# Hybrid attention and RWKV block: attention in steps of one segment, output products six steps back, every fifth full segment transposed by TensorE

## The chip, the cores and the metric

The kernel runs on one core of a Trainium2 chip. The metric is the device time of one execution in microseconds, lower is better. The core's engines work in parallel, each through its own queue in order: TensorE (PE, whose weight loads show as PEld), VectorE (DVE), ScalarE (ACT), GpSimd (POOL), and SyncE (SP), which here only issues transfers. ACT and POOL issue transfers too, and the 16 DMA engines carry all of them.

## What is computed

One block over 4096 tokens plus 16 meta tokens, with 8 attention heads of width 64 beside 8 RWKV-7 heads, then an output projection and a norm. The attention part of the reference, shortened:

```python
s = einsum('bhqd,bhkd->bhqk', q, k) / sqrt(64) + cq[..., :, None] - ck[..., None, :]
s = where(k_pos <= q_pos, s, NEG_INF)
o = einsum('bhqk,bhkd->bhqd', softmax(s), v)     # per block of 128 queries
y_fox = o * silu(z)
h = h + concatenate([y_fox, y_rwkv]) @ w_out     # then the final RMSNorm
```

## The kernel before

The program has two parts. In the **first part** the RWKV recurrence runs in 129 chunks of 32 tokens, three hops each. After each hop some of the input projections are put in as filler: a generator `fill` goes through four passes over the 16 blocks of 256 tokens (pass 0 makes the RWKV inputs, pass 1 the Q, K, V and gate of head pair 2, pass 2 those of pairs 0 and 1, pass 3 those of pair 3 and the RWKV gate). Each hop adds `RATE` = 0.33 to a credit; a yield of the generator costs 0.25 for 12 matmuls of 256 columns, so one unit is 48 such matmuls (`ps_in`, `ps_qk`, `ps_vz`, `ps_zr`).

In the **second part** the heads run in the order `HEADS`. A head has 32 rows of 128 queries; row i sees W = 16 + 128(i+1) keys, cut into segments of `SEG` = 1024. That makes 52 full segments and 32 shorter ones per head, 416 and 256 in all. For each segment:

1. PE makes the scores in a PSUM tile `ps_q` (two buffers): two matmuls of up to 512 columns for the high and low half of Q, and a mask product on the diagonal.
2. DVE adds the forget bias and takes the running maximum, into `sp` (fp32, L1051).
3. When all segments of the row have their maximum, ACT takes the exponential in place (L1065) and copies it to fp16, the high half of `hl` (L1071). POOL or DVE, by `POOL_SHARE` = 60 in 100, subtracts to get the low half (L1076).
4. SP issues a DMA transpose of `hl` (128 x 2048 fp16 for a full segment) into `ht` (L1078).
5. PE multiplies each 128 keys of `ht` with V: one matmul of 128 columns and one of 64, in `ps_o`.

`advance` takes one row at a time: all scores of row n, then all output products of row n-1 (`finish`), then steps 3 and 4 for all segments of row n. The buffers are 9 of `sp`, 6 of `hl` and 6 of `ht`. Between rows the rest of the filler is put in, in proportion to work done: what is left of `fill` counts in units, then `rwkv_out` (32 rows of 24 matmuls of 512 columns, `ps_p`) counts 0.5 a row. During head 7 the output projection and norm of finished rows run (`out_prep`, `out_rows`, again 24 `ps_p` matmuls a row).

A scheduler sets the order in every queue from priorities (`PR`) and its own model of time; an engine's queue is in order on the chip. `Ordered` can pin an instruction behind another one: in mode "note" it remembers the last instruction, in mode "behind" it adds an order-only dependency on it.

Of the kernel before, what the change touches and what calls it, by code (L numbers as in the profile page):

```python
# [40 lines left out]
NHL, NSP = 6, 9  # L41
HEADS = (4, 5, 0, 1, 2, 3, 6, 7)
POOL_SHARE = 60
# [4 lines left out]
RATE = 0.33  # L48
LEAD = 6
PARTS = ((0, 0), (0, 1), (1, 0))  # L50
# [26 lines left out]
def hymba_kernel(ctx: ExitStack, tc, x, meta, norm_w, w_in, b_f, mu_shift, w0, w_up, a0, a_up,  # L77
# [884 lines left out]
    with ExitStack() as fs:  # L962
# [18 lines left out]
        def projected(p, t):  # L981

            while done[PASS_OF[p]] * NB < min(t, SEQ + 1):
                next(late)
# [26 lines left out]
        nseg = 0  # L1011
        qz = {}

        def attention(h, i, head, dst):

            nonlocal nseg
            p, hp = divmod(h, 2)
            q0 = 64 * hp
            if i % 4 == 0:
                g = min(4, NT - i)  # L1020
                t0 = N_META + i * P
                projected(p, t0 + g * P)
                Q = at.tile([P, 2, 4 * P], F16, tag="Q", name="Q")
                for a in range(2):
                    DQ.dma_start(Q[64 * a:64 * a + 64, :, :g * P],
                                 qk_d[p][a:a + 2, q0:q0 + 64, t0:t0 + g * P].rearrange("v p t -> p v t"))
                Zt = at.tile([P, 4, HD], F32, tag="Z", name="Zt")
                DQ.dma_start(Zt[:, :g], zf_d[p][t0:t0 + g * P, q0:q0 + 64].rearrange("(s t) e -> t s e", t=P))
                qz[h] = (Q, Zt)
            Q, Zt = qz[h]  # L1030
            W = N_META + P * (i + 1)
            qs = slice((i % 4) * P, (i % 4) * P + P)
            sps = []
            mt = at.tile([P, 8], F32, tag="mt", name="mt", bufs=4)
            ni = 0
            for a0 in range(0, W, SEG):
                sp = at.tile([P, SEG], F32, tag="sp", name="sp", bufs=NSP)
                sps.append(sp)
                for a in range(a0, min(a0 + SEG, W), 1024):
                    b = min(a + 1024, W)  # L1040
                    c, o = chunk(a)
                    o = a - o
                    ps = ps_q.tile([P, 1024], F32, tag="q", name="ps_q")
                    for a2 in range(a, b, 512):
                        b2 = min(a2 + 512, b)
                        dg = max(a2, min(b2, W - P))
                        for v in range(2):
                            mm(ps[:, a2 - a:b2 - a], Q[:, v, qs], head[c][0][:, a2 - o:b2 - o], v == 0, v == 1 and dg == b2)
                        if dg < b2:
                            mm(ps[:, dg - a:b2 - a], identb, dmask[:, dg - W + P:b2 - W + P], False, True)  # L1050
                    V.tensor_tensor_reduce(out=sp[:, a - a0:b - a0], in0=ps[:, :b - a], in1=head[c][2][:, a - o:b - o],  # L1051
                                           scale=scs[:, p, 0, hp:hp + 1],
                                           scalar=(-3e38 if ni == 0 else mt[:, ni - 1:ni]),
                                           op0=ALU.add, op1=ALU.max, accum_out=mt[:, ni:ni + 1])
                    ni += 1
            nm = at.tile([P, 8], F32, tag="nm", name="nm", bufs=8)
            V.tensor_scalar(out=nm[:, 0:1], in0=mt[:, ni - 1:ni], scalar1=-1.0, scalar2=P_SHIFT,  # L1057
                            op0=ALU.mult, op1=ALU.add)
            yield
            hts = []  # L1060
            for a in range(0, W, SEG):
                b = min(a + SEG, W)
                n = b - a
                sp = sps[a // SEG]
                A.activation(sp[:, :n], sp[:, :n], AF.Exp, bias=nm[:, 0:1], accum_out=nm[:, 1 + a // SEG:2 + a // SEG])  # L1065
                nt = -(-n // P)
                hl = at.tile([P, 2 * SEG], F16, tag="hl", name="hl", bufs=NHL)[:, :2 * nt * P]
                hl3 = hl.rearrange("p (a k) -> p a k", a=2)
                if n % P:
                    G.memset(hl3[:, :, n:], 0.0)  # L1070
                A.activation(hl3[:, 0, :n], sp[:, :n], AF.Copy)  # L1071
                eng = V
                if n > P:
                    nseg += 1
                    eng = G if nseg * POOL_SHARE % 100 < POOL_SHARE else V
                eng.tensor_tensor(out=hl3[:, 1, :n], in0=sp[:, :n], in1=hl3[:, 0, :n], op=ALU.subtract)  # L1076
                ht = at.tile([P, 2 * SEG // P, P], F16, tag="ht", name="ht", bufs=NHL)[:, :2 * nt]
                SP.dma_start_transpose(out=ht, in_=hl)  # L1078
                hts.append(ht)
            yield  # L1080
            pso = ps_o.tile([P, P], F32, tag="o", name="ps_o")
            for a, ht in zip(range(0, W, SEG), hts):
                b = min(a + SEG, W)
                n = b - a
                nt = -(-n // P)
                for j in range(nt):
                    k = min(P, n - j * P)
                    jt = a // P + j
                    c, o = chunk(a + j * P)
                    Vj = head[c][1][:, o // P]  # L1090
                    first, last = jt == 0, b == W and j == nt - 1
                    mm(pso, ht[:k, j], Vj[:k], first, False)
                    mm(pso[:, 0:HD], ht[:k, nt + j], Vj[:k, 0:HD], False, last)
            ns = len(sps)
            if ns > 1:
                V.tensor_reduce(out=nm[:, 1:2], in_=nm[:, 1:1 + ns], axis=mybir.AxisListType.X, op=ALU.add)
            V.reciprocal(nm[:, 7:8], nm[:, 1:2])
            o1 = at.tile([P, HD], F32, tag="o1", name="o1", bufs=4)
            A.activation(o1, pso[:, HD:], AF.Copy)
            V.tensor_tensor(out=o1, in0=pso[:, 0:HD], in1=o1, op=ALU.add)  # L1100
            V.scalar_tensor_tensor(out=dst, in0=o1, scalar=nm[:, 7:8], in1=Zt[:, i % 4],
                                   op0=ALU.mult, op1=ALU.mult)
            yield

        heads = {h: {} for h in range(8)}
        need = lambda i: chunk(N_META + P * (i + 1) - 1)[0]

        def fetch(x, i):

            for (xx, ii) in ((x, i), (x, min(i + 3, NT - 1)), (min(x + (i + 6) // NT, 7), (i + 6) % NT)):  # L1110
                for c in range(need(ii) + 1):
                    if c not in heads[HEADS[xx]]:
                        heads[HEADS[xx]][c] = head_load(HEADS[xx], c)

        def out_weights(ow, k0):

            OH = ow.tile([P, 4, D], F32R, name="OH")
            OL = ow.tile([P, 4, D], F32R, name="OL")
# [167 lines left out]
```

## Time and profile before

| | |
|---|---|
| time, median of 3 runs (lowest to highest) | 4504.49 us (4469.48 to 4522.03) |
| the profiled execution: its time, and its span | 4462.28 us, 4460.4 us |
| busy over the span: PE, DVE, ACT, POOL | 88%, 66%, 48%, 50% |
| mean granted TensorE clock | 0.916 of full speed |
| full segments and shorter segments of attention | 416 and 256 |
| DMA transposes `ht<-hl` | 672 |

The span is that of one profiled execution, and the rows below are of that one. The last matmul of the recurrence (`psz`) starts at 1982 us and the first score (`ps_q`) at 2122 us, so these cut the program into its parts; the last score starts at 4319 us. Busy PE time counts each matmul from its start to its modelled end, so matmuls that follow each other closely overlap. A DMA share is packet time over 16 engines' time, and packets of several queues overlap, so it can pass 1.

### The profile page before, as it was taken

What the parts mean: (1) busy time and instruction counts of PE and PEld (TensorE: products, weight loads), DVE (VectorE), ACT (ScalarE), POOL (GpSimd) and SP (SyncE); (2) the same over time, 40 slices, a digit from 0 to 9 for tenths busy, and PEclk for the clock granted to TensorE, in tenths of its full rate; (3) what the DMA queues carried; (4) which work ended last, traced back from release to release, by engine and by line L of the source; (5) the groups of instructions that cost most, each with busy time, mean ns of one, the idle gap of its engine ahead of it and who ended that gap; (6) DMA issues with size and microseconds to landing.
All of it is one profiled execution on the core that took longest, in us unless ns stands there. A gap on an engine that the chain in (4) does not pass through costs nothing. (4 is left out here: it accounts for less than half of the span.)

```text
span 4460.4 us, 106426 instructions
## 1 busy us (share of the span) xinstructions
PE 3912.1 (88%) x42336; PEld 3012.8 (68%) x42336; DVE 2956.9 (66%) x6217; ACT 2122.7 (48%) x4338; POOL 2230.5 (50%) x3289
## 2 busy tenths in 40 slices
PE   5689999999989899998878878888888878978888
PEld 4577777777767677777656655666666656666566
DVE  5346665666667666752878978677787758646774
ACT  5433333333333233321666757577676747524552
POOL 4137565667666665762445545444454435332340
PEclk8899999999876899899999989999999989989989
DMA  9963223323222344324999999999999999999995
GB/s 265 262 172 93 79 79 97 87 75 90 74 70 79 85 138 121 98 88 141 196 213 229 216 193 227 199 216 227 208 212 234 212 203 223 258 270 242 198 218 185
DMA packets 1702644, 755.37 MB, mean 169 GB/s; under 512 B 1444601, under 2 KB 1639601, under 8 KB 1692162
## 3 DMA queue, kind: packets, MB, share of 16 engines
q1 hardware_dynamic: 1489346, 502.84, 55.8%
q10 hardware_dynamic: 194624, 170.08, 15.3%
q0 software_dynamic: 18176, 75.66, 5.6%
q8 instruction: 332, 5.44, 0.5%
q14 instruction: 166, 1.36, 0.1%
HBM read 278.97 MB, written 158.50 MB: 98 GB/s over the span
## 5 line engine op out<-in xcount | busy, mean ns | idle before, releaser
L1076 POOL TENSOR_TENSOR hl<-sp,hl 128x1024 f16<-128x1024 f32 (+7 forms) x384 | 719.7, 1881 | 517.3 <-ACT hl L1071 440.7
L1065 ACT ACTIVATE sp<-sp,nm 128x1024 f32<-128x1024 f32 (+8 forms) x672 | 644.5, 962 | 223.5 <-DVE nm L1057 175.6
L1071 ACT ACTIVATE hl<-sp 128x1024 f16<-128x1024 f32 (+8 forms) x672 | 568.2, 872 | 366.1 <-DMA ht<-hl 239.4
L92 PE MATMUL ps_o<-Vt,ht 128*128 128x64 f16 (+3 forms) x8960 | 559.5, 211 | 180.6 <-DMA ht<-hl 177.8
L92 PE MATMUL ps_q<-K,Q 128*128 128x512 f16 (+4 forms) x2432 | 596.9, 366 | 119.4 <-DVE mt L1051 118.3
L758 POOL TENSOR_TENSOR tm<-X,Am 128x248 f32<-128x248 f32 (+30 forms) x1023 | 498.1, 487 | 376.6 <-DMA Am<-a_d 290.1
L92 PEld LDWEIGHTS <-ht 128*128 128x128 f16 (+1 forms) x8960 | 466.9, 100 | 315.0 <-DMA ht<-hl 204.9
L92 PEld LDWEIGHTS <-wu 128*128 128x128 f16 (+1 forms) x5476 | 513.1, 102 | 194.8 <-ACT wu L160 28.1
L760 POOL TENSOR_TENSOR X<-X,tm 128x248 f32<-128x248 f32 (+30 forms) x1023 | 517.7, 506 | 76.6
L67 PEld LDWEIGHTS <-wu 128*128 128x128 f16 (+1 forms) x4988 | 454.5, 101 | 114.3 <-issue 26.0
L1051 DVE CUSTOM_DVE_ANT_0 sp<-ps_q,cb,mt 128x1024 f32<-128x1024 f32 (+8 forms) x416 | 436.1, 1048 | 80.3 <-PE ps_q L92 40.8
L1076 DVE TENSOR_TENSOR hl<-sp,hl 128x1024 f16<-128x1024 f32 (+8 forms) x288 | 383.2, 1333 | 99.3 <-ACT hl L1071 98.1
L92 PEld LDWEIGHTS <-Q 128*128 128x128 f16 x2432 | 221.8, 100 | 294.8 <-issue 150.2
L67 PE MATMUL ps_in<-fu,wu 128*128 128x256 f16 x3108 | 416.0, 285 | 3.4 <-DVE car L67 3.4
L1051 DVE CUSTOM_DVE_ANT_0 sp<-ps_q,cb,scs 128x1024 f32<-128x1024 f32 (+7 forms) x256 | 297.6, 1164 | 71.2 <-POOL hl L1076 43.9
L92 PE MATMUL ps_qk<-fu,wu 128*128 128x256 f16 x1632 | 237.7, 280 | 24.0 <-DVE t1k L500 18.5
L92 PE MATMUL ps_vz<-wu,fu 128*128 128x256 f16 x1644 | 247.6, 284 | 1.0 <-ACT th L544 0.6
L92 PE MATMUL ps_p<-OH,yH 128*128 128x512 f32 x512 | 221.5, 433 | 29.0 <-DVE oxt L1144 27.5
L1070 POOL MEMSET hl<- 128x224 f16 x256 | 72.4, 287 | 336.8 <-DMA ht<-hl 318.4
L92 PE MATMUL ps_zr<-fu,wu 128*128 128x256 f16 x1536 | 224.8, 285 | 8.0 <-DVE nm L1057 6.3
L67 PE MATMUL psz<-UV,SC 32*64 32x64 f32 (+1 forms) x4128 | 222.4, 232 | 3.0 <-ACT UV L67 2.2
L92 PE MATMUL ps_p<-OH,yL 128*128 128x512 f32 x512 | 209.6, 411 | 0.0
(350 smaller groups left out, 6976.6 us busy)
## 6 DMA issues: line engine op xcount, KB each, us to landing
fu<-u_d POOLq DMA_DIRECT2D x32, 1024.0 KB, 6.8
fu<-u_d SPq DMA_DIRECT2D x30, 1024.0 KB
pr<-p_d SPq DMA_DIRECT2D x32, 832.0 KB
p_d<-prt SPq DMA_DIRECT2D x96, 256.0 KB
u_d<-u SPq DMA_DIRECT2D x16, 1024.0 KB
Am<-a_d SPq DMA_DIRECT2D x128, 128.0 KB
Q<-qk_d ACTq DMA_DIRECT2D x128, 128.0 KB
oxt<-in_x_dram ACTq DMA_DIRECT2D x32, 512.0 KB
```

The lines of the kernel that those rows point to most:

```text
L67: r = f(*args, **kw)
L92: PE.matmul(o, lhsT=l, rhs=r, start=start, stop=stop)
L758: G.tensor_tensor(out=tm[:, :, :k], in0=bc(X[:, :, s:s + 1], [P, 8, k]), in1=bc(Am[:, s * C + s + 1:s * C + C].unsqueeze(1), [P, 8, k]), o ...
L760: G.tensor_tensor(out=X[:, :, s + 1:], in0=X[:, :, s + 1:], in1=tm[:, :, :k], op=ALU.add)
L1051: V.tensor_tensor_reduce(out=sp[:, a - a0:b - a0], in0=ps[:, :b - a], in1=head[c][2][:, a - o:b - o], scale=scs[:, p, 0, hp:hp + 1], scala ...
L1065: A.activation(sp[:, :n], sp[:, :n], AF.Exp, bias=nm[:, 0:1], accum_out=nm[:, 1 + a // SEG:2 + a // SEG])
L1070: G.memset(hl3[:, :, n:], 0.0)
L1071: A.activation(hl3[:, 0, :n], sp[:, :n], AF.Copy)
L1076: eng.tensor_tensor(out=hl3[:, 1, :n], in0=sp[:, :n], in1=hl3[:, 0, :n], op=ALU.subtract)
```

## The change

- Attention goes in steps of one segment. Step (n, sg) makes the scores of segment sg of row n+1, then the weights (exponential, split, transpose) of segment sg of row n, and then the output products of the segment that stands `LAG` = 6 steps back in a list `pend`.
- PE's order is tied: the first output matmul of a step is pinned behind the last score matmul.
- Of the full segments every fifth (`PE_SHARE` = 20) is not split into `hl` and not transposed by DMA. PE transposes its fp32 weights from `sp` in eight pieces of 128 x 128 into a `ps_q` buffer (`ps_w`); ACT copies the high half out to `ht`, and DVE subtracts for the low half.
- `RATE` falls from 0.33 to 0.265; 4 units of filler (`AHEAD`) go ahead of attention; `rwkv_out` counts 1.0 a row, not 0.5, and fill that a head forces is counted as spent.
- Buffers: `sp` 9 to 7, `hl` 6 to 5, `ht` 6 to 9, `nm` 8 to 12, `o1` 4 to 2, `Zt` 2 to 3. The share of POOL in the subtractions goes from 60 to 75 in 100. Q of the next four rows is loaded two rows ahead. Rows of the output projection follow what `pend` has finished.

```diff
-NHL, NSP = 6, 9
+NHL, NSP, NHT = 5, 7, 9
+PE_SHARE = 20
-POOL_SHARE = 60
+POOL_SHARE = 75
+AHEAD = 4
-RATE = 0.33
+RATE = 0.265
+LAG = 6
...
+        def weights(n, sg):
...
+            A.activation(sp[:, :nn], sp[:, :nn], AF.Exp, bias=nm[:, 0:1], accum_out=nm[:, 1 + sg:2 + sg])
+            ht = at.tile([P, 2 * SEG // P, P], F16, tag="ht", name="ht", bufs=NHT)[:, :2 * nt]
+            r["hts"].append(ht)
+            if nn == SEG:
+                npe += PE_SHARE
+                if npe >= 100:
+                    npe -= 100
+                    pt = ps_q.tile([P, nt, P], F32, tag="q", name="ps_w")
+                    for j in range(nt):
+                        PE.transpose(pt[:, j], sp[:, j * P:(j + 1) * P], ident)
+                    A.activation(ht[:, :nt], pt, AF.Copy)
+                    V.tensor_tensor(out=ht[:, nt:], in0=pt, in1=ht[:, :nt], op=ALU.subtract)
+                    return
...
+        def output(n, sg):
...
+            PE.mode = "behind"
+            for j in range(nt):
...
+                mm(pso, ht[:k, j], Vj[:k], jt == 0, False)
+                PE.mode = None
+                mm(pso[:, 0:HD], ht[:k, nt + j], Vj[:k, 0:HD], False, jt * P + k == W)
...
-                    yield 0.5
+                    yield 1.0
...
+        def pipeline():
+
+            for n in range(-1, len(steps)):
+                ka = segs(n) if n >= 0 else 0
+                kb = segs(n + 1) if n + 1 < len(steps) else 0
+                for sg in range(max(ka, kb)):
+                    if sg < kb:
+                        PE.mode = "note"
+                        scores(n + 1, sg)
+                        PE.mode = None
+                    if sg < ka:
+                        weights(n, sg)
+                        pend.append((n, sg))
+                    while len(pend) > LAG or pend and pend[0][0] < n - 4 or (n == len(steps) - 1 and sg == ka - 1 and pend):
+                        output(*pend.pop(0))
+                    if sg < ka:
+                        yield n, min(SEG, width_of(steps[n][1]) - sg * SEG) + 2 * P // ka
...
+        with tc.high_priority(offset=PR[5]):
+            while spent < AHEAD:
+                spent += next(late)
+        while now < 7 * NT:
+            with tc.high_priority(offset=PR[3]):
+                now, cols = next(att)
+            work += cols
+            with tc.high_priority(offset=PR[5]):
+                while spent * allwork < work * left:
```

Two places in the built program. First, ACT's queue where the recurrence gives way to attention: `qk`, `vt` and `t1k` end filler units, `Yt` ends the last RWKV rows, and the DMA rows load the first heads' K, bias, V and Q. Before:

```order
L67 ACTIVATE vt<-ps_vz 128x4x64
L67 ACTIVATE t1k<-t1k 128x256
L67 ACTIVATE qk<-ps_qk,sqs 128x256
L67 ACTIVATE qk<-ps_qk 128x256
L492 ACTIVATE vt<-ps_vz 128x4x64
L891 ACTIVATE Yt<-psd,gbT,gwT 128x32 x4
L502 ACTIVATE t1k<-t1k 128x256
L995 DMA K<-qk_d_102 64x1024 x3
L995 DMA K<-qk_d_102 64x1040
```

And in the changed kernel at the same place:

```order
L882 ACTIVATE sqd<-Y 32x512
L495 ACTIVATE vt<-ps_vz 128x4x64
L70 ACTIVATE wu<-wst 128x8x128
L505 ACTIVATE t1k<-t1k 128x256
L894 ACTIVATE Yt<-psd,gbT,gwT 128x32 x4
L999 DMA K<-qk_d_102 64x1024 x2
L1001 DMA cb<-c_d 128x1024
L1005 DMA Vt<-v_d_106 128x8x128
L1043 DMA Q<-qk_d_102 64x2x512 x4
L1045 DMA Zt<-zf_d_110 128x4x64 x3
L999 DMA K<-qk_d_102 64x1024 x2
```

The long run of filler ahead of `Yt` is gone: on PE 1074 `ps_qk` and `ps_vz` matmuls stand between the last `psz` and the first `ps_q` before, 120 now. Ahead of the last `psz` stand 2040 before and 1704 now, behind the first `ps_q` (with `ps_zr`) 4950 before and 6240 now. After the last `ps_q` stand 420 `ps_p` before and 300 now.

Second, PE in head 0 at the row of 1024 + 144 keys: score matmuls are `ps_q`, output products `ps_o`, and `fu` weights belong to filler. Before:

```order
L92 LDWEIGHTS Q
L92 MATMUL ps_q<-K,Q 128x512
L92 LDWEIGHTS Q
L92 MATMUL ps_q<-K,Q 128x144
L92 LDWEIGHTS Q
L92 MATMUL ps_q<-K,Q 128x144
L92 LDWEIGHTS ht
L92 MATMUL ps_o<-Vt,ht 128x128
L92 LDWEIGHTS identb
L92 MATMUL ps_q<-dmask,identb 128x128
L92 LDWEIGHTS ht
L92 MATMUL ps_o<-Vt,ht 128x64
```

And now, around the first segment that PE transposes:

```order
L1105 MATMUL ps_w<-ident,sp 128x128
L70 LDWEIGHTS Q
L70 MATMUL ps_q<-K,Q 128x512
L70 LDWEIGHTS Q
L70 MATMUL ps_q<-K,Q 128x512
L70 LDWEIGHTS Q
L70 MATMUL ps_q<-K,Q 128x144
L70 LDWEIGHTS Q
L70 MATMUL ps_q<-K,Q 128x144
L70 LDWEIGHTS identb
L70 MATMUL ps_q<-dmask,identb 128x128
L1105 MATMUL ps_w<-ident,sp 128x128 x7
```

Output products no longer stand among the matmuls of one score segment. The first of the eight transposes stands ahead of the next scores, the other seven behind them. In all 83 segments go this way (664 `ps_w`), and SP issues 589 transposes instead of 672.

## Rows read from the trace of the kernel before

**Rows 1.** The page: span, and busy time by engine (share, instructions).

```profile
span 4460.4 us, 106426 instructions
PE 3912.1 (88%) x42336; PEld 3012.8 (68%) x42336; DVE 2956.9 (66%) x6217; ACT 2122.7 (48%) x4338; POOL 2230.5 (50%) x3289
```

**Rows 2.** Busy by stage: from:to, length, busy (instructions), PE clock, DMA share, GB/s.

```profile
core 0: us, PE busy (x) PEld busy (x) DVE busy (x) ACT busy (x) POOL busy (x), PEclk, DMA share, GB/s
300.00:1982.00 1682.00, 1615.57 (x20914) 1269.92 (x20915) 1079.23 (x2363) 551.06 (x1374) 1111.51 (x2188) 0.91 0.32 89
1982.00:2122.00 140.00, 121.02 (x1097) 107.01 (x1094) 37.94 (x99) 20.80 (x53) 38.77 (x60) 0.93 0.45 140
2122.00:2833.00 711.00, 589.52 (x6240) 431.57 (x6238) 595.85 (x1251) 490.89 (x932) 363.28 (x343) 0.93 1.12 213
2833.00:3593.00 760.00, 661.32 (x6877) 499.02 (x6876) 563.29 (x1202) 509.24 (x1003) 352.67 (x330) 0.94 1.15 217
3593.00:3926.00 333.00, 270.30 (x2317) 197.77 (x2314) 216.77 (x438) 182.74 (x350) 134.21 (x116) 0.90 1.14 224
3926.00:4319.00 393.00, 330.61 (x2343) 242.25 (x2342) 250.88 (x482) 193.65 (x352) 132.67 (x110) 0.92 1.09 235
4319.00:4461.00 142.00, 119.53 (x649) 94.80 (x647) 72.47 (x106) 39.32 (x71) 21.88 (x25) 0.94 0.63 194
```

**Rows 3.** DMA queues, 2122 to 4461: packets, MB, share; an issue with its count.

```profile
q1 hardware_dynamic: 1168384, 293.69, 73.7%
q10 hardware_dynamic: 179408, 158.23, 27.2%
q0 software_dynamic: 13568, 55.79, 8.3%
...
fu<-u_d POOLq DMA_DIRECT2D x23, 1024.0 KB, 7.8
```

**Rows 4.** PE's waits, 2122 to 4461: for whom, us in total, times, longest.

```profile
PE ps_o L92 <- DMA ht<-hl: 177.8, 87, 11.0
PE ps_q L92 <- DVE mt L1051: 118.3, 104, 7.1
PE ps_p L92 <- DVE oxt L1144: 27.5, 19, 5.4
```

**Rows 5.** PE and ACT in order of time, 1982 to 2122: start, us, work, count.

```profile
1993.77 5.40 PE L67 MATMUL ps_vz<-wu,fu 128*128 128x256 f16 x48
...
2112.83 4.30 PE L92 MATMUL ps_qk<-fu,wu 128*128 128x256 f16 x20 [18.50 <-DVE t1k L500]
...
2084.62 8.52 ACTq L995 DMA_DIRECT2D K<-qk_d  x10
...
2109.76 1.17 ACTq L1028 DMA_DIRECT2D Zt<-zf_d  x2
```

**Rows 6.** PE in order of time, inside head 3.

```profile
3013.64 1.03 PE L92 MATMUL ps_q<-K,Q 128*128 128x512 f16 x4
...
3016.24 0.84 PE L92 MATMUL ps_o<-Vt,ht 128*128 128x128 f16 x16
```

**Rows 7.** The chain that ended last: one row of the output projection.

```profile
4414.67 5.72 PE ps_p L92 x24
```

**Rows 8.** The fp32 transposes that the kernel already has, with what empties them: ns min/median/max.

```profile
L1233 PE MATMUL ps_t<-ident,yf x128: 269/273/476, 4090.1 to 4440.7; 128*128 128x128 f32 x128
L1129 ACT ACTIVATE yH<-ps_t x32: 571/597/600, 4091.2 to 4441.0; 128x512 fp32r<-128x512 f32 x32
L1130 DVE TENSOR_TENSOR yL<-ps_t,yH x32: 671/691/693, 4091.8 to 4441.6; 128x512 fp32r<-128x512 f32 x32
...
4090.08 1.09 PE L1233 MATMUL ps_t<-ident,yf 128*128 128x128 f32 x4 [3.26 <-issue]
...
4420.23 0.60 PE L1233 MATMUL ps_t<-ident,yf 128*128 128x128 f32 x4
```

**Rows 9.** Groups by line and form, 2122 to 4461: busy us, mean ns, idle before.

```profile
L1076 POOL TENSOR_TENSOR hl<-sp,hl 128x1024 f16<-128x1024 f32 x240 | 532.6, 2223 | 412.3 <-ACT hl L1071 338.6 <-issue 29.8 <-DMA fnw<-in_final_norm_w_dram 19.6
L1065 ACT ACTIVATE sp<-sp,nm 128x1024 f32<-128x1024 f32 x416 | 473.6, 1140 | 172.0 <-DVE nm L1057 144.5 <-DVE ss L181 4.3 <-DMA out_dram<-oxt 4.2
...
L1051 DVE CUSTOM_DVE_ANT_0 sp<-ps_q,cb,mt 128x1024 f32<-128x1024 f32 x216 | 289.1, 1339 | 41.1 <-PE ps_q L92 27.8 <-POOL hl L1076 4.6 <-DVE mt L1051 3.0
L1076 DVE TENSOR_TENSOR hl<-sp,hl 128x1024 f16<-128x1024 f32 x176 | 271.5, 1543 | 53.3 <-ACT hl L1071 52.4 <-DMA Zt<-zf_d 0.6
```

More of the change, by code (lines that the diff above doesn't have):

```diff
@@ L981, in projected @@
         def projected(p, t):
+            nonlocal spent
             while done[PASS_OF[p]] * NB < min(t, SEQ + 1):
-                next(late)
+                spent += next(late)
         def head_load(h, c):
@@ L1009, in chunk @@
             return c, x - c * CH
[L1011 to L1103, printed above, removed]
@@ L1105, in hymba_kernel @@
+        nseg, npe, spent = 0, 0, 0
+        steps = [(hx, i) for hx in range(8) for i in range(NT)]
+        rows = {}
+        width_of = lambda i: N_META + P * (i + 1)
+        segs = lambda n: -(-width_of(steps[n][1]) // SEG)
+        qz, yos = {}, {}
         heads = {h: {} for h in range(8)}
-        need = lambda i: chunk(N_META + P * (i + 1) - 1)[0]
+        need = lambda i: chunk(width_of(i) - 1)[0]
         def fetch(x, i):
@@ L1169, in filler @@
                 for _ in rwkv_out(op, OW):
[L1170 to L1173 removed]
+                    yield 1.0
+        left = sum(max(0, NFULL - done[i]) * n for i, n in ((1, 2), (2, 4), (3, 4))) + NT
         late = filler()
[L1175 to L1189 removed]
@@ L1191, in advance @@
-        def advance(hx, i):
-            nonlocal before, yo
-            h = HEADS[hx]
-            fetch(hx, i)
-            if i % 4 == 0:
-                yo = at.tile([P, 4, HD], F32, tag="yo", name="yo")
-            gen = attention(h, i, heads[h], yo[:, i % 4])
-            next(gen)
-            finish()
-            next(gen)
-            before = h, i, gen, yo
-        yo = None
-        for hx in range(7):
-            for i in range(NT):
-                with tc.high_priority(offset=PR[3]):
-                    advance(hx, i)
-                work += i + 2
-                with tc.high_priority(offset=PR[5]):
-                    while spent * 7 * NT * (NT + 3) < work * 2 * total:
-                        cost = next(late, None)
-                        if cost is None:
-                            break
-                        spent += cost
+        pend = []
@@ new lines, in hymba_kernel @@
+        att = pipeline()
+        work, now = 0, -1
+        allwork = 7 * sum(width_of(i) + 2 * P for i in range(NT))
+        with tc.high_priority(offset=PR[5]):
+            while spent < AHEAD:
+                spent += next(late)
+        while now < 7 * NT:
[4 more added lines that the diff above has]
+                while spent * allwork < work * left:
+                    cost = next(late, None)
+                    if cost is None:
+                        break
+                    spent += cost
```

146 lines of the change are left out of this document (119 added, 27 removed).

## The prediction

> **What bounds the kernel now.** I read the page's shares first, then the stages, then inside attention PE's waits and the DMA queues. The page gives PE 88% of the span and every other engine 66% or less [rows 1]. That is an average over two parts with different limits. In the first part, 300 to 1982 us, PE is busy 1615.6 of 1682 us (96%) while the DMA engines stand at 0.32 [rows 2]: PE bounds it. From 1982 to 2122 us PE is busy 121.0 us with nothing but projections, DVE 37.9 and ACT 20.8: a seam in which attention hasn't begun. From 2122 us to the end PE is busy 83%, 87%, 81%, 84% and 84% of the five stages, while the DMA share is 1.09 to 1.15 until 4319 us. DVE is next, 1699 us of 2338 in sum (73%).
>
> Busy time there hides holes, since it counts the drain after each run of matmuls. So I count PE's work by pitch. A full segment's scores are four matmuls, 1.03 us with some 0.17 us of drain, so 0.86 us; 128 keys of output products are 0.084 us (16 matmuls, 0.84 us, the same drain) [rows 6]; a filler matmul is 0.109 us (48 in 5.40 us) [rows 5]; a row of the output projection 5.72 us [rows 7]. By the loops: scores 416 x 0.86 = 358, and 256 shorter segments at some 0.45 (464 columns twice, and the mask) = 115; products 4480 x 0.084 = 376; filler 4950 x 0.109 = 540; `rwkv_out` and output projection 64 x 5.72 = 366; small transposes 15. Sum 1770 us of the 2338. Named waits are 177.8 us of products for the transposes `ht<-hl`, 118.3 us of scores for DVE, which frees the two `ps_q` buffers, and 27.5 us of the output projection [rows 4], 324 in all. The other 244 us are mostly the half-speed clock: 0.93 granted over 2338 us is some 160 us, the rest small holes. The DMA engines are close behind: `q1`, nearly all of it transposes, holds 73.7% alone [rows 3].
>
> **The change, part by part.** *First part.* Ahead of the last `psz` 2040 `qk`/`vz` matmuls fall to 1704. 336 x 0.109 = 37 us, on the path because PE is 96% busy. Bounds: 0, if the recurrence's own hops set the pace, and 73 us at half speed (20 in 4.30 us, 0.215 each [rows 5]). I take -37.
>
> *Seam.* 1074 matmuls fall to 120: 954 x 0.109 = 104 us. What stays is ACT's queue. It issues 27 loads for the first heads from 2084.6 to 2110.9 us [rows 5], and PE then waits 18.5 us for what is queued behind them on ACT. The change puts eleven at the front, with the K, bias and Q of the first scores; at 26.3/27 = 0.97 us each that is 11 us, then their landing. So the seam is 30 to 80 us instead of 140; I take 45: -95.
>
> *Filler moved into attention.* 1290 matmuls x 0.109 = +141 us, up to 152 at the granted 0.93. Its loads, of 1024 KB a block, grow by 1290/192 = 7 to the 23 there [rows 3]; with their results that is some 15 MB, and at `q0`'s price (8.3% of 2338 us for 55.8 MB) 50 us of all engines' time. `rwkv_out` at 1.0 a row only spreads over seven heads what now stands mostly in head 6, so nothing for it.
>
> *TensorE transposes.* 83 segments leave the DMA queue: 83 x 0.524 MB = 43.5 of 293.7 MB, 15% of `q1`, 255 us of DMA time. PE gets 664 transposes. Four like them took 0.60 us at full speed, 0.109 apart, and 1.09 us at half speed, at most 0.27 each [rows 8]: 72 to 181 us. I take 0.128, near the lower because that is the full-speed row: +85. Emptying a buffer takes ACT 2 x 0.59 = 1.2 us against 1.05 now, and DVE 2 x 0.69 = 1.4 us. DVE's other subtractions fall from 288 to 171 (-117 x 1.54 at most), so DVE loses some 40 us or more; POOL's rise from 384 to 418, +34 x 2.2 = 75 us on an engine busy 1005 us of 2338 [rows 2, 9]. Both lie beside PE.
>
> The row shows 0.109 to 0.27 us for one fp32 transpose on PE [rows 8]. The Trainium skill, "VectorE: DVE Perf Modes", section "The three transpose paths", puts one 128 x 128 transpose at 390 ns on TensorE and 1309 ns by the DMA crossbar. By its first figure the 664 would cost 259 us, an estimate, and the total would be 174 us higher than mine; the trace disagrees, in a row of transposes they overlap.
>
> *Six steps of lag.* Today products of row n-1 follow directly on the scores of row n, and six `ht` buffers have to serve two rows. With six steps between transpose and product (a step is some 3.5 us of PE work) about 20 us pass; the longest wait now is 11.0 us. So of 177.8 us I take -160, bounds 0 and -178. This needs DMA engines that keep up: 2567 share-us in the five stages (share x length, summed) less 255 plus 50 is 2362, and over the length forecast below that is 1.04 against 1.10 now.
>
> *Scores a segment at a time, tied.* Today a row's up to five score segments compete for two buffers, which DVE empties at 1.34 us each against 0.86 us of PE work [rows 9]. In steps, products and filler stand between. Of 118.3 us I take -80, bounds 0 and -118. The output projection's waits: -20 of 27.5, because 300 instead of 420 `ps_p` are left after the last score. Fewer waits leave fewer half-speed slots: of 160 us I take -60 (bounds 0 and -110).
>
> *A new wait.* The `ps_w` transposes wait for the exponential (1.14 us) and hold one of the two `ps_q` buffers until DVE's subtraction ends; next scores are queued behind them on PE, and DVE waits for those. Nothing in the trace has this. Bounds: 0 if other work stands ready, and the whole chain each time, 1.14 + 0.85 + 1.2 + 1.4 = 4.6 us, 380 us in all. The nearest row is the scores' wait for a buffer, 118.3 us in 104 times; I take 0.4 us each, +35. The smaller pools (`sp`, `hl`) cost nothing as long as ACT (61%) and POOL (43%) have room; without it they would show as DVE waiting for POOL.
>
> **Sum.** Stretch from 2122: +141 + 85 - 160 - 80 - 20 - 60 + 35 = -59. Span: 4460 - 37 - 95 - 59 = 4269, and 2 us lie around it: 4271, say 4270 us. The three runs shown have their median at 4504, 42 us above the profiled one, so against the median it is 5% less. Both floors lie below: PE's work 1770 + 226 = 1996 at 0.93 is 2146 us for the stretch, DMA at today's 1.10 is 2147 us, and I forecast 2279.
>
> **Rivals.** *All waits go.* If lag and ties clear everything named, the stretch falls to its floors, some 2150: 4460 - 37 - 95 - 188 + 2 = 4142 us. For it: both floors agree, and 324 us are named. Against: two resources this near each other seldom both run full. Chance 0.22.
>
> *Half relief.* DMA queueing keeps half of the transposes' waits, and scores still wait for DVE: 4270 + 71 + 80 = 4421 us. For it: DMA stays above 1.0, and DVE nears 75%. Chance 0.13.
>
> *It doesn't do what it says.* The waits put down to the transposes are really for a low half that comes late from POOL (it idles 412 us ahead of these, then takes 2.2 us each [rows 9]), and more goes to POOL now. Then no wait shrinks and PE gains 226 us: 4460 - 37 - 95 + 226 - 20 + 2 = 4536 us, no change that shows. Against: a lag would cover this too. Chance 0.07.
>
> *Slower.* PE stands at each `ps_w` for the whole chain, as its first transpose ahead of the next scores makes possible: 4270 - 35 + 380 = 4615 us. It decides from 3.8 us each: (4549 - 4235)/83. Against: scheduled order mostly puts other work between. Chance 0.05.
>
> **How the numbers follow.** My forecast has 0.53, with 4200 to 4350 as its own range. The range 4090 to 4430 leaves out the two last rivals (0.12) and the best of the first. Faster by over 1%, about what a measurement of this kernel can tell from no change (below 4459): 0.53 + 0.22 + 0.13 = 0.88; within 1%: 0.07; slower: 0.05.
>
> **What would show it.** Right: first `ps_q` near 1990 us; 589 DMA transposes; PE's wait for `ht<-hl` under 40 us and for DVE's maximum under 60; DMA share near 1.04; clock in attention 0.95 or more; `ps_w` in 0.9 to 1.2 us for eight. Wrong: PE waiting on ACT's exponential ahead of `ps_w` for over 100 us in sum, `ht` waits above 100 us, or a first score later than 2050 us.

## The result and the profile after

The changed kernel takes 4503.86 us (median of 20 runs, 4472.39 to 4542.44) beside 4468.85 us for the kernel before (20 runs, 4429.80 to 4522.03). The ratio is 1.0091, interval [1.0066, 1.0117]: slower by 0.9%, where 5% less was forecast. Single executions of either kernel spread over some 2%, so differences of 20 us between two profiles prove little; ratios over many runs do.

The page's shares answer [rows 1]; the span is 41 us longer.

```profile
span 4501.4 us, 107381 instructions
## 1 busy us (share of the span) xinstructions
PE 3961.7 (88%) x43000; PEld 3076.2 (68%) x43000; DVE 2952.4 (66%) x6184; ACT 2121.1 (47%) x4338; POOL 2270.6 (50%) x3322
```

The stages answer [rows 2]. The first part now ends at 1964 us and the first score starts at 1987 us:

```profile
core 0: us, PE busy (x) PEld busy (x) DVE busy (x) ACT busy (x) POOL busy (x), PEclk, DMA share, GB/s
300.00:1964.00 1664.00, 1578.85 (x20581) 1236.28 (x20580) 1071.70 (x2333) 547.17 (x1362) 1092.28 (x2171) 0.91 0.31 88
1964.00:1987.00 23.00, 16.63 (x136) 13.83 (x136) 12.53 (x27) 4.62 (x10) 8.25 (x15) 0.85 0.56 151
1987.00:4502.00 2515.00, 2162.03 (x20368) 1655.71 (x20368) 1731.30 (x3545) 1434.12 (x2759) 1093.34 (x1018) 0.94 0.94 194
```

The first part gives back 18 us and the seam 117 (23 instead of 140). Attention with its tail takes 2515 us; the five attention stages of [rows 2] add up to 2339 us with PE busy 1971. So the stretch grew by 176 us: PE's busy time by 191, while its idle time, length less busy, went from 368 to 353 us. Nearly all of the waiting that the change was to remove is still there.

PE's waits in attention answer [rows 4] (for whom, us in total, times, longest):

```profile
PE ps_q L70 <- DVE mt L1079: 105.7, 66, 6.5
PE ps_o L70 <- DMA ht<-hl: 64.6, 31, 7.7
PE ps_w L1105 <- ACT sp L1096: 51.5, 21, 11.1
PE ps_p L95 <- DVE oxt L1192: 37.9, 25, 6.8
PE ps_vz L70 <- DVE t1k L503: 16.1, 1, 16.1
PE ps_q L70 <- DVE ht L1107: 14.6, 13, 2.1
PE ps_zr L95 <- DVE t1k L503: 9.7, 4, 8.1
```

The wait for transposes fell from 177.8 to 64.6 us, and the maximum's only from 118.3 to 105.7. The others rose, or are new: the seven rows add up to 300 us, beside 324 for the three of [rows 4]; with every smaller wait counted it is 342 us beside 357. Most of the wait moved from one operand to another.

The DMA queues of the same stretch answer [rows 3], with the count of transposes behind:

```profile
q1 hardware_dynamic: 995744, 250.16, 59.3%
q10 hardware_dynamic: 184360, 162.24, 24.2%
q0 software_dynamic: 17312, 71.59, 10.0%
...
fu<-u_d POOLq DMA_DIRECT2D x30, 1024.0 KB, 7.5
...
ht<-hl SPq DMA_TRANSPOSE x589
```

83 transposes and 43.5 MB left `q1`, and seven filler loads came, as forecast. The DMA share went from 1.10 to 0.94, lower than the 1.04 forecast, and PE's idle time hardly moved with it.

TensorE's new transposes, and what empties them (ns: least, median, longest), answer [rows 8]:

```profile
L1105 PE MATMUL ps_w<-ident,sp x664: 270/273/477, 2041.3 to 4401.1; 128*128 128x128 f32 x166
L1106 ACT ACTIVATE ht<-ps_w x83: 999/1018/1038, 2047.1 to 4407.2; 128x1024 f16<-128x1024 f32 x83
L1107 DVE TENSOR_TENSOR ht<-ps_w,ht x83: 1205/1215/1226, 2049.3 to 4409.7; 128x1024 f16<-128x1024 f32 x83
```

Their size was right: seven in a row take 0.93 us (PE in order of time), which is 0.27 for the last and 0.11 for each ahead of it, so 664 at 0.109 cost some 72 us.

```profile
2042.00 0.93 PE L1105 MATMUL ps_w<-ident,sp 128*128 128x128 f32 x7
```

### The profile page after: what moved, and what is told of

Its sections match the earlier page's. It is cut to its first block, busy times and chain, and to the rows that moved or that the text cites. A ratio compares the mean times of both kernels' runs of the same rounds, so it can differ in the third digit from the quotient of the medians.

```text
span 4501.4 us, 107381 instructions
## 1 busy us (share of the span) xinstructions
PE 3961.7 (88%) x43000; PEld 3076.2 (68%) x43000; DVE 2952.4 (66%) x6184; ACT 2121.1 (47%) x4338; POOL 2270.6 (50%) x3322
## 5 line engine op out<-in xcount | busy, mean ns | idle before, releaser
L1118 POOL TENSOR_TENSOR hl<-sp,hl 128x1024 f16<-128x1024 f32 (+7 forms) x417 | 774.5, 1873 | 479.5 <-ACT hl L1113 449.1
L70 PE MATMUL ps_q<-K,Q 128*128 128x512 f16 (+4 forms) x2432 | 597.2, 365 | 124.2 <-DVE mt L1079 105.7
L1113 ACT ACTIVATE hl<-sp 128x1024 f16<-128x1024 f32 (+8 forms) x589 | 471.1, 843 | 163.8 <-DMA ht<-hl 109.9
L95 PE MATMUL ps_o<-Vt,ht 128*128 128x64 f16 (+2 forms) x8288 | 522.3, 209 | 0.4 <-DVE ht L1107 0.4
L95 PEld LDWEIGHTS <-ht 128*128 128x128 f16 (+1 forms) x8288 | 433.6, 100 | 79.1 <-issue 12.9
L95 PE MATMUL ps_vz<-wu,fu 128*128 128x256 f16 x2040 | 284.7, 279 | 6.0 <-DVE qk L478 3.1
L95 PE MATMUL ps_qk<-fu,wu 128*128 128x256 f16 x1992 | 277.7, 277 | 7.2 <-DVE t1k L503 4.8
L1118 DVE TENSOR_TENSOR hl<-sp,hl 128x1024 f16<-128x1024 f32 (+8 forms) x172 | 244.9, 1428 | 41.0 <-ACT hl L1113 40.7
L95 PEld LDWEIGHTS <-fu 128*128 128x128 f16 x2232 | 202.1, 100 | 37.7 <-issue 7.2
L70 PE MATMUL ps_o<-Vt,ht 128*128 128x128 f16 (+1 forms) x672 | 149.9, 225 | 71.7 <-DMA ht<-hl 64.6
```

The lines of the kernel that those rows point to most:

```text
L70: r = f(*args, **kw)
L95: PE.matmul(o, lhsT=l, rhs=r, start=start, stop=stop)
L1113: A.activation(hl3[:, 0, :nn], sp[:, :nn], AF.Copy)
L1118: eng.tensor_tensor(out=hl3[:, 1, :nn], in0=sp[:, :nn], in1=hl3[:, 0, :nn], op=ALU.subtract)
```

## The experiments

"Before" and "after" are the two kernels; each ratio is to the kernel before, with its 95% interval. Attention windows run from the first score to the end; idle is their length less PE's busy time.

**Filler.** First RATE alone, in either kernel. `b_rate265` is before with the new rate:

```diff
-RATE = 0.33
+RATE = 0.265
```

> The kernel before with RATE 0.265 and nothing else. Theory P: the seam shrinks by some 100 us and attention grows by as much, time within 25 us of before, ratio 0.995 to 1.005. Rival G (filler hides in PE's 463 us of holes in attention): ratio 0.970 to 0.985. Rival F (filler in attention costs more): ratio 1.01 to 1.02.

Measured: 1.0095 [1.0061, 1.0128], as much as the whole change, and nearest to Rival F. The profile shows where: the first part ends 23 us earlier and the seam is 48 instead of 140 us, but attention is 143 us longer, 125 of it PE's busy time.

```profile
300.00:1959.00 1659.00, 1572.76 (x20580) 1232.14 (x20577) 1072.13 (x2332) 546.49 (x1361) 1090.44 (x2170) 0.91 0.32 88
1959.00:2007.00 48.00, 27.24 (x217) 22.43 (x218) 19.43 (x40) 7.17 (x16) 12.22 (x21) 0.79 0.64 179
2007.00:4489.00 2482.00, 2095.87 (x19626) 1576.34 (x19624) 1776.68 (x3566) 1430.27 (x2754) 1045.44 (x979) 0.94 1.02 212
```

Some 1210 more matmuls stand in attention. They do not fall into its holes: idle is 386 us instead of 368. `a_rate33` gives after the old rate, `a_rate40` and `b_rate40` more.

```diff
-RATE = 0.265
+RATE = 0.33
```

> The changed kernel with RATE back at 0.33, so that more filler stands in the first part and at the seam and less in attention. Theory P (filler costs PE the same wherever it stands): within 20 us of the changed kernel, ratio to the kernel before 1.004 to 1.014. Rival F (filler in attention costs more than its 0.109 us a matmul, since it displaces scores that DVE and ACT wait for): attention shorter by more than the seam grows, ratio 0.98 to 0.998. Rival G (filler in attention hides in waits): ratio 1.02 to 1.03.

> The changed kernel with RATE 0.40 instead of 0.265. Theory F: the same slope as between 0.265 (1.0091) and 0.33 (1.0033), ratio to the kernel before 0.992 to 1.000, attention shorter than with 0.33 by some 25 us more than the seam is longer. Rival: ratio 1.001 to 1.010, as heads without filler have nothing to put into their waits.

> The kernel before with RATE 0.40 instead of 0.33, so that still more filler stands in the first part and at the seam and less in attention. Theory F (a filler matmul costs more in attention than at the seam, by some 0.03 us, as 0.265 against 0.33 showed with +0.95%): ratio 0.988 to 0.997. Rival (the gain ends at 0.33, since heads then run without filler to cover their waits): ratio 1.000 to 1.012.

Measured: `a_rate33` 1.0033 [1.0003, 1.0062], `a_rate40` 1.0057 [1.0025, 1.0090], `b_rate40` 0.9965 [0.9929, 1.0001]. `a_rate33` fell between its two theories; `a_rate40` is the rival's. So 0.6% of after's 0.9% goes with the rate, and beyond 0.33 nothing sure is to be had.

**TensorE's share.** `a_noshare` is after with all transposes by DMA; `b_share` is before with every fifth full segment transposed by TensorE, without the tie.

```diff
-PE_SHARE = 20
+PE_SHARE = 0
```

> The changed kernel with no segment transposed by TensorE (PE_SHARE 0); all 672 transposes go by DMA again. Theory P (PE's work in order decides, the transposes are pure addition): 72 us of PE work by pitch and the 52 us and 15 us of waits at ps_w and for DVE's ht go, some 40 us of waits for ht<-hl come back, so the span falls from 4501 to about 4400 us, ratio to the kernel before 0.975 to 0.990, waits of ps_o for ht under 110 us. Rival D (the relief of the DMA engines pays for them): the waits for ht<-hl go back to 178 us or more, DMA share in attention back to 1.05 or more, span 4480 to 4540 us, ratio 1.000 to 1.015.

```diff
+                if n == SEG:
+                    npe += 20
+                    if npe >= 100:
+                        npe -= 100
...
+                        for j in range(nt):
+                            PE.transpose(pt[:, j], sp[:, j * P:(j + 1) * P], ident)
+                        A.activation(ht[:, :nt], pt, AF.Copy)
+                        V.tensor_tensor(out=ht[:, nt:], in0=pt, in1=ht[:, :nt], op=ALU.subtract)
+                        hts.append(ht)
+                        continue
```

> The kernel before with every fifth full segment transposed by TensorE and nothing else. Theory M (a wait taken away in attention comes back at another place, so that only PE's work counts): PE's waits for ht<-hl fall from 177.8 us to 90 to 130 us, 72 us of work by pitch and some 50 us of waits at ps_w are added, ratio 0.997 to 1.012. Rival D (the DMA relief is a gain of its own): ratio 0.975 to 0.993.

Measured: `a_noshare` 1.0139 [1.0089, 1.0189], in Rival D's range, so in steps of a segment the share at least does no harm. `b_share` 1.0423 [1.0375, 1.0472]: in row order and without the tie it costs 4.2%, outside both expectations. PE's waits in attention of `b_share`:

```profile
PE ps_o L92 <- DMA ht<-hl: 277.8, 116, 19.0
PE ps_q L92 <- DVE mt L1051: 74.6, 62, 5.3
PE ps_w L1074 <- ACT sp L1065: 58.9, 21, 6.3
```

With a fifth of the transposes gone, PE waits longer for the rest. The new `ps_w` row is the smaller part of it. ACT shows another: it stands before it can copy a finished row out of `ps_o`, and the exponentials and splits of later rows are queued behind that copy. From 2122 to 4461 us, in before and in `b_share`:

```profile
ACT o L1099 <- PE ps_o L92: 48.2, 37, 7.8
```

```profile
ACT o L1111 <- PE ps_o L92: 253.2, 90, 19.2
```

So late products can hold up the next weights, and these the next products. No run here opens that loop, so it is not shown to be the cause of the 4.2%.

**The tie.** `a_notie` takes it out of after, `b_tie` puts it into before.

```diff
-            PE.mode = "behind"
+            PE.mode = None
```

> The changed kernel without the tie: no output matmul is pinned behind a score matmul. Theory P: the tie sets the order of work that PE has to do anyway, ratio to the kernel before 1.000 to 1.020, waits of ps_q for DVE's maximum 80 to 150 us. Rival T (the tie makes PE stand at scores whose buffer DVE still holds while products could run): those waits fall below 70 us and the ratio to 0.985 to 0.998.

```diff
+            PE.mode = "note"
...
+                    PE.mode = "behind" if first else None
                     mm(pso, ht[:k, j], Vj[:k], first, False)
+                    PE.mode = None
```

> The kernel before with the tie alone: the first output matmul of row n-1 is pinned behind the last score matmul of row n; rows, lag and buffers as before. Theory O (the order of scores ahead of products is what the change brought; without it the changed kernel was 2% slower): PE's waits of ps_q for DVE fall from 118.3 us, ratio to the kernel before 0.975 to 0.995. Rival (the tie helps only with products six steps back; here it holds products, and with them the six ht buffers, behind a whole row of scores): ht buffers come free later, ratio 1.005 to 1.03.

Measured: `a_notie` 1.0299 [1.0253, 1.0346], the largest single price within after and more than I had expected; `b_tie` 0.9975 [0.9942, 1.0008], between its two theories. The rows of `a_notie` show that the tie works on the products, not on the scores: `ht` waits of 233.0 instead of 64.6 us, the maximum's 99.5 beside 105.7.

```profile
PE ps_o L95 <- DMA ht<-hl: 233.0, 89, 20.5
PE ps_q L70 <- DVE mt L1079: 99.5, 58, 8.3
```

**The lag.** `a_lag2` has two steps, `a_lag8` eight (with one `ht` buffer more, and one `hl` less to make room).

```diff
-LAG = 6
+LAG = 2
```

> The changed kernel with products two steps back instead of six. Theory L: two steps are some 8 us against 13.3 us in the median from exponential to landed transpose, so most products wait, PE's waits for ht<-hl rise from 64.6 us to 250 us or more, ratio to the kernel before 1.035 to 1.08. Rival (the scheduler puts the products late enough in any case, by its own model of time): ht waits 60 to 130 us, ratio 1.005 to 1.02.

```diff
-NHL, NSP, NHT = 5, 7, 9
+NHL, NSP, NHT = 4, 7, 10
...
-LAG = 6
+LAG = 8
```

> The changed kernel with products eight steps back instead of six, 10 ht buffers instead of 9 and 4 hl instead of 5 (the three pools fill what room there is). Theory L (six steps, 21.5 us from exponential to product in the median, are shorter than the slow tenth of the way from exponential to landed transpose, 23.0 us): PE's waits for ht<-hl fall from 64.6 us to under 35, time 25 to 50 us less than the changed kernel, ratio to the kernel before 0.998 to 1.004. Rival: four hl buffers hold the splits back, ACT's wait for ht<-hl rises above 110 us, ht waits stay above 60 us, ratio 1.007 to 1.020.

Measured: 1.0220 [1.0158, 1.0283] and 1.0162 [1.0087, 1.0238]. Eight steps, with one `hl` less, thus buy nothing. With two steps PE waits 193.2 us for `ht`, 129 more than with six, but loses only 1.3% of the time, some 58 us: less than Theory L said, more than its rival. The built programs tell why the lag matters so little. Over all 672 segments, count the later score tiles that stand in PE's queue ahead of a segment's first output product: the median is **13 in the kernel before, 10 in the changed one**, 8 without the tie, 7 with two steps, 11 in `a_noshare`, and 13 in `b_tie`. The scheduler had already put the products further back than the code reads; steps with LAG = 6 shortened that distance, and the tie gave part of it back. In time, from the start of a full segment's exponential to the start of its first product, the median is 25.6 us before and 21.2 after (traced segment by segment, those that go by DMA).

**Which side of PE.** `a_pool100` and `a_pool50` move the subtractions between DVE and POOL; `a_later` makes the `ps_w` transposes one step later, behind that step's scores.

```diff
-POOL_SHARE = 75
+POOL_SHARE = 100
```

> The changed kernel with all subtractions of more than 128 columns on POOL instead of 75 in 100; DVE loses some 139 of them, about 200 us. Theory V (scores wait for a ps_q buffer because DVE is late with other work): PE's waits of ps_q for DVE fall from 120 us to under 80, ratio to the kernel before 0.995 to 1.005. Rival W (the buffer pair and the order make the wait, and POOL makes the low half later): ps_q waits stay above 100 us, ht waits rise above 90 us, ratio 1.010 to 1.025.

> The changed kernel with POOL_SHARE 50 in place of 75, so a third fewer subtractions on POOL and the others on DVE. In the changed kernel SP's queue waits 593 us for POOL's low halves, in one case 105.6 us. Theory L (late low halves on POOL delay the transposes, and with them PE): ht waits fall from 65 to below 40 us, ratio to the kernel before 0.99 to 1.003. Rival M (SP's waiting is slack that the six steps cover, and DVE's maxima are what pays): waits of scores for DVE's maximum rise from 106 to over 120 us, ratio 1.005 to 1.02.

```diff
-                    pt = ps_q.tile([P, nt, P], F32, tag="q", name="ps_w")
-                    for j in range(nt):
-                        PE.transpose(pt[:, j], sp[:, j * P:(j + 1) * P], ident)
...
+                    turned.append((sp, ht, nt))
...
+                    turn()
```

> The changed kernel with TensorE's transposes put one step later, pinned behind that step's scores, so that the exponential they need has ended. Theory P: PE's wait of ps_w for the exponential falls from 51.5 us to under 15 and the time by 30 to 50 us, ratio to the kernel before 0.998 to 1.003. Rival: the ps_q buffer is then held when the next scores want it, the wait moves to ps_q for DVE's ht (14.6 us now, then over 40), ratio 1.006 to 1.015.

Measured: 1.0149 [1.0092, 1.0207] with all of them on POOL, 1.0054 [1.0024, 1.0083] with half. DVE's load of subtractions alone isn't what makes PE wait for the maximum: with none above 128 columns on DVE that wait is 142.9 us. And with fewer on POOL the `ht` wait falls to 45.2 us while the maximum's rises to 136.2, as Rival M said; the ratio is 0.4% below after's, with intervals that just overlap. Whether SP's waits for low halves are slack this run doesn't show, since they mostly changed sides: SP waits 628 us for POOL's and 216 for DVE's in after, 344 and 388 here. `a_later` is 1.0097 [1.0053, 1.0142]: the `ps_w` waits fall from 51.5 to some 22 us, those for `ht` rise to 90.4 and those for the maximum to 123.1, and the time stays.

**Work taken out.** In `a_skip` and `b_skip` nobody transposes the fifth of the segments, and their products read a constant tile. `b_skip` has no tie, whatever its expectation says: its edit differs from that of `b_share` in the transposes and in that constant tile alone.

```diff
+        hs = at.tile([P, 1, P], F16, tag="hs", name="hs", bufs=1)
+        V.memset(hs, 0.0)
...
+                    r["hts"].append(None)
+                    return
...
-                mm(pso, ht[:k, j], Vj[:k], jt == 0, False)
+                mm(pso, hs[:k, 0] if ht is None else ht[:k, j], Vj[:k], jt == 0, False)
```

> The changed kernel, but every fifth full segment (83 of 416) is transposed by nobody: neither TensorE nor the DMA queue, no split, and its output products read one small constant tile instead of its weights. So it leaves out the transposes of those segments and their weights in the result. It tells what the relief of the DMA queue is worth when PE pays nothing for it. Theory P (the change is slow because PE pays 72 us of transposes and 51 us of standing ahead of ps_w): both come back nearly whole, ratio to the kernel before 0.975 to 0.988, PE's ht waits near 60 us. Rival N (the holes between PE's pieces are made by the order of the queues as a whole, and work taken out of PE turns into holes): ratio 0.995 or more, ht and DVE-maximum waits together 40 us or more above the changed kernel's 170.

> The kernel before with the tie, and every fifth full segment transposed by nobody, its products reading one small constant tile (so it leaves out those segments' transposes and weights). Against the same kernel with TensorE doing these transposes (1.042) it tells whether the row order suffers from ps_w on PE or from what stands behind it. Theory P (PE's ps_w in a row-wise order holds the score buffers and PE, and that alone makes the 4%): ratio 0.95 to 0.98, DMA share below 1.0, ht waits below 130 us. Rival N (relief of the DMA queue is worth nothing in a row-wise order since the row's other transposes still end it): 0.985 to 1.00, ht waits 160 us or more.

Measured: 1.0032 [1.0013, 1.0051] and 0.9852 [0.9817, 0.9886]. From after, 72 us of PE's work and 51.5 us of `ps_w` waits are gone, yet only 0.6% of the time: in its rows the other waits have taken their place, 279 us in two of them beside 170 in after. Both ratios are in Rival N's range. In row order the same work out is worth 5.7 points (1.0423 to 0.9852), far more than those 72 us.

```profile
1999.00:4481.00 2482.00, 2100.15 (x19706) 1588.32 (x19704) 1669.39 (x3462) 1359.38 (x2676) 1084.57 (x1018) 0.93 0.94 196
```

```profile
PE ps_q L70 <- DVE mt L1081: 151.8, 105, 11.5
PE ps_o L70 <- DMA ht<-hl: 126.8, 53, 9.7
```

So PE's own added work is not what kept the forecast from coming. `a_nolow` and `b_nolow` (this one has the tie) leave out the low halves: no subtraction for segments that go by DMA, half the bytes in each transpose, PE's work unchanged.

```diff
-            eng.tensor_tensor(out=hl3[:, 1, :nn], in0=sp[:, :nn], in1=hl3[:, 0, :nn], op=ALU.subtract)
-            SP.dma_start_transpose(out=ht, in_=hl)
+            SP.dma_start_transpose(out=ht[:, :nt], in_=hl)
...
-                mm(pso[:, 0:HD], ht[:k, nt + j], Vj[:k, 0:HD], False, jt * P + k == W)
+                mm(pso[:, 0:HD], hs[:k, 0] if low is hs else ht[:k, nt + j], Vj[:k, 0:HD], False, jt * P + k == W)
```

> The changed kernel without the low halves of the segments that go by DMA: no subtraction for them (so POOL's 775 us and DVE's 245 us at L1118 are gone), the DMA transposes are half as large, and the low products read one small constant tile. It leaves those low halves out of the result; PE's work is the same to the instruction. Theory D (the holes on PE are made by the path behind the exponential: copy, subtraction, SP's queue, transpose, and its buffers): PE's ht waits below 20 us, DVE-maximum waits below 60 us, ratio to the kernel before 0.955 to 0.975. Theory M (they are made ahead of it, by the round trip from a score through DVE's maximum to ACT's exponential and the next score's buffer): ht waits fall too, but the maximum's and ps_w's waits stay at 150 us or more in sum, ratio 0.985 to 1.00.

> The kernel before with the tie, without any low halves: no subtraction at L1076, DMA transposes half as large, the low products read one small constant tile. It leaves the low halves out of the result; PE's work is the same. Theory D (the path behind the exponential sets the row-wise kernel's holes): ht waits below 50 us and ratio 0.94 to 0.965; more than by taking a fifth of the segments off that path (0.985). Theory M (the maximum's round trip does): ht waits fall, the maximum's waits stay above 110 us, ratio 0.975 to 0.99.

Measured: 0.9482 [0.9451, 0.9512] and 0.9371 [0.9339, 0.9404]; the medians are 4243.70 and 4199.84 us. Attention of `a_nolow`, then of `b_nolow`:

```profile
1982.00:4229.00 2247.00, 2088.89 (x20368) 1626.15 (x20368) 1358.81 (x3373) 1428.91 (x2759) 296.90 (x601) 0.97 0.73 161
```

```profile
2129.00:4190.00 2061.00, 1888.84 (x18417) 1431.13 (x18414) 1229.06 (x3188) 1397.23 (x2704) 254.68 (x538) 0.97 0.80 177
```

With the same 20368 matmuls as after, the stretch is 268 us shorter: idle falls from 353 to 158 us, and the same work is busy 73 us less, at a clock of 0.97 instead of 0.94. Both runs gained more than Theory D's range, although PE's waits for `ht` fell less than it said (39.2 us against 20, 78.6 against 50). PE's waits in `a_nolow`:

```profile
PE ps_q L70 <- DVE mt L1081: 57.3, 30, 6.6
PE ps_o L70 <- DMA ht<-hl: 39.2, 10, 12.5
...
PE ps_w L1108 <- ACT sp L1098: 8.6, 3, 4.5
```

The waits named for the maximum and for the exponential fall too, from 105.7 to 57.3 and from 51.5 to 8.6 us, although nothing was done to the scores, the maxima or the exponentials. So the larger part of those waits followed from the path behind the exponential. How much of the gain belongs to the subtractions and how much to the halved transposes stays open, since these runs drop both. They also take load off DVE, which makes the maxima (busy 1731 us in after, 1359 in `a_nolow`); `a_pool100` speaks against that as the cause, since it took most subtractions off DVE and the maximum's wait rose, but SP's waits for POOL's low halves rose with it (866 us, 628 in after).

`b_best` joins what came out below 1 in before, the tie and the rate of 0.40:

```diff
-RATE = 0.33
+RATE = 0.40
```

> The kernel before with the tie and with RATE 0.40: the two edits that alone gave 0.9975 and 0.9965. If they add: 0.994 (0.990 to 0.998), seam 50 to 60 us instead of 140. Rival (they share one gain, or the fuller first part takes it back): 0.997 to 1.001.

Measured: 0.9957 [0.9926, 0.9987], median 4456.86 us, in the range for two gains that add. It has the lowest ratio of the kernels here with all of the computation in them, 0.4% under before and some 1.3% under the changed kernel, but isn't told apart from `b_rate40`.

## Why the prediction was wrong

**The 5%.** The sum of 4270 us was built on an execution of 4460 us; like for like it is 4.3% less. The rest of the 5% is the distance to a median of three runs, 4504 us, which over 20 runs is 4469.

**Seam and first part.** The seam's mechanism was right, its size not: forecast 45 us with bounds of 30 and 80, measured 23. The first part gave back 18 us, not 37. Together that is -135 against -132, two misses of some 20 us that cancel by luck. The error isn't here.

**Filler moved, transposes.** Right in size. The transposes cost 72 us by the rows above, +85 forecast. The filler's +141 is still the product 1290 x 0.109, but `b_rate265` bears it out: 125 us more busy time for some 1210 matmuls. The sentence on `rwkv_out` was wrong: it did not spread over seven heads (the first `ps_p` stands at 3641 us of the 4501).

**Waits.** This is where the forecast failed. It summed -160, -80, -20 and +35 to -225 us; the named waits went from 324 to 300, -24. By term: the transposes' wait fell 113 us (-160 forecast), the maximum's 13 (-80), the output projection's rose 10 (-20), and the new waits came to 92 us instead of 35: `ps_w` 51.5, scores held by `ps_w`'s subtraction 14.6, and filler held by DVE 25.8. The half-speed clock, forecast at -60, went from 0.93 of 2339 us to 0.94 of 2515: 164 to 151 us, -13. So of 285 us that waits and clock were to give, 37 came; the largest misses are the maximum's (67) and the new waits (57), then the transposes' and the clock's (47 each). The sum 141 + 72 - 24 - 13 = 176 is the stretch's measured growth. That it meets to the microsecond is luck: with every smaller wait counted the -24 is -15, and a clock read to two digits leaves some 12 us open in each of its terms.

The first step that failed is the one on the lag: "about 20 us pass; the longest wait now is 11.0 us". It compared the new distance with the longest *wait*, not with the distance that the products already had. That was 25.6 us and 13 score tiles, more than the new 21.2 us and 10. I had read "products of row n-1 follow directly on the scores of row n" from the code; the built order of PE's queue tells otherwise, and could have been counted beforehand. The wait for `ht` did shrink, by 113 of the 160 us, but for another reason than the one given: from the start of its exponential a segment's transpose now lands (the last step of its semaphore) in a median of 14.1 us instead of 22.5. The share has part in that (`a_noshare`: 19.0 us, `ht` waits 149.8), and the waits also need the tie (`a_notie`: 233.0) and the lag (`a_lag2`: 193.2).

The second failure is the larger one, and the maximum's -80 is its plainest case: I subtracted each wait as if PE would gain it. Three experiments took a wait or work out of PE and saw it come back under another name, in part (`a_lag2` against after, `a_skip`) or whole (`a_later`). `a_nolow` and `b_nolow` show what the waits hang on: with the low halves gone, 195 of 353 us of PE's holes go, the maximum's among them. So most of the holes are made behind the exponential, in the split and the transposes that feed PE. The prediction looked at this path through the DMA share alone ("DMA engines that keep up", 1.04); that share fell to 0.94 and the holes stayed.

**The signs named.** First score near 1990 us (1987), 589 DMA transposes and 0.9 to 1.2 us for eight `ps_w` came as forecast. `ht` waits below 40 us (64.6), the maximum's below 60 (105.7), a clock of 0.95 (0.94) and a DMA share near 1.04 (0.94) did not. Of the three signs named for wrong none showed, although the forecast was: they watched single waits, and the waits had moved.

**The rivals.** "All waits go" and "half relief" end on the same wrong side as the forecast. "It doesn't do what it says" (4536 us) came nearest in time; the outcome lies in the band within 1%, which had a chance of 0.07. It put the waits down to low halves that come late, and `a_nolow` bears out that the split and its transposes make them; but its condition that no wait shrinks did not hold (the `ht` row fell by 113 us), and moving subtractions from POOL to DVE changed little (`a_pool50`). "Slower" by standing at `ps_w` is wrong: 51.5 us in 21 waits, 0.6 us for each of the 83 segments where it needed 3.8.

**The transpose page.** The Trainium skill, "VectorE: DVE Perf Modes", section "The three transpose paths", has 390 ns for a transpose on TensorE (of bf16; these are fp32). The trace disagrees here too: 0.109 us apart, a median of 273 ns from start to end of one.

**What the change is, by parts.** The rate costs about 0.6 to 0.95% (`a_rate33`, `b_rate265`). Steps with tie and lag buy nothing over the row order that can be measured: with the rate of 0.265 and no share, the segment-wise kernel stands at 1.0139 and the row-wise one at 1.0095, with overlapping intervals. TensorE's transposes cost 4.2% in row order and nothing that can be measured within after (0.5% less with them, intervals that overlap). Whether the steps or the tie make them bearable is not shown, since `b_share` has neither: row order with tie and share was not run, and steps with share but no tie stand at 1.0299. And little is to be had from a fifth: taken off the path at no cost at all it is worth 1.5% (`b_skip` against before).

## What to carry to other kernels

Before pricing a lag, count in the built queue how far back the consumer already stands: the source says in which order work is asked for, not in which it runs. A named wait on an in-order engine is not a sum to be had; ask which path feeds it, and test that by taking work out of the path while the engine's own work stays the same. Filler moved from a dense stretch into one with holes added its full length there (`b_rate265`); the holes don't take it up by themselves.

## What the runs showed of the hardware

How long a transpose holds SP's queue, which issues it (ns: least, median, longest), in before, after, `a_nolow` and `b_nolow`:

```profile
L1078 SPq DMA_TRANSPOSE ht<-hl x672: 1167/2134/12831, 2125.6 to 4347.2; - x168
```

```profile
L1119 SPq DMA_TRANSPOSE ht<-hl x589: 1167/1903/24923, 2013.7 to 4412.9; - x197
```

```profile
L1116 SPq DMA_TRANSPOSE ht<-hl x589: 1119/1234/7645, 2007.4 to 4127.6; - x197
```

```profile
L1076 SPq DMA_TRANSPOSE ht<-hl x672: 1119/1241/5215, 2132.3 to 4037.9; - x168
```

Summed over the trace, SP is held 1800 of 2339 us before, 1481 of 2515 after, and 989 of 2061 in `b_nolow`. So a queue that "only issues" was held for 77%, 59% and 48% of attention, and a transpose behind a long hold starts late. In before a hold has a mean of 1.79 us when no packet of `q10` or `q0` starts in it, and of 2.8 to 3.4 us, by how many start in a microsecond, when some do; part of that gap is only that a longer hold has more chance to meet a packet. The Trainium skill, "DMA: Bandwidth & Descriptors", section "Queues, rings and completion order", says that each DMA engine takes turns between the queues it has work for; the trace agrees in direction, and no run here changed the other queues' load to prove it. The DMA share did not tell how well PE was fed: at 1.10 and at 0.94 it idled about the same, 368 and 353 us.
